# Keeping a split weight for a second use, and moving 24 matmuls ahead: two edits to a two-layer hybrid trunk

## The chip, the core and the metric

The kernel runs on one core of one Trainium2 chip. The metric is the device time of one launch in microseconds (us); lower is better. The engines of the core are TensorE (PE, matmuls), VectorE (DVE), ScalarE (ACT), GpSimd (POOL) and SyncE (SP, which issues the DMA loads). Each works through its own list of instructions in the order in which the program was built.

## The reference, cut to what matters

Two layers over 1024 rows of width 1024, everything in float32. Each layer is a token mixer (layer 0: a state-space mixer, layer 1: a short gated convolution) and then an MLP; each sub-layer is normalised, shifted, scaled, gated and added to the residual stream.

```
def short_conv_mixer(h, in_w, conv_w, out_w):
    proj = h @ in_w
    Bg, Cg, xv = jnp.split(proj, 3, axis=-1)
    y = Bg * causal_dwconv(Cg * xv, conv_w)
    return y @ out_w

def sqrelu_mlp(h, up_w, down_w):
    a = jax.nn.relu(h @ up_w)
    return (a * a) @ down_w
...
        h = rmsnorm(x, mlp_norm_w[i]) * (1.0 + sc_f) + sh_f
        x = x + g_f * sqrelu_mlp(h, mlp_up[i], mlp_down[i])
```

`mlp_up` is 1024 x 4096, `mlp_down` 4096 x 1024.

## The kernel before, in words

**Precision.** A float32 product is made of three matmuls: weight high part times activation high part, weight low part times activation high part, and a bf16 copy of the weight times the activation's low part. So each 128-column strip of a weight (a `wraw` tile, 128 x 1024, loaded by SP) is split in three: `split3` (L776) does a cast on ACT (`whi`, L783), a subtraction on DVE (`wlo`, L784) and a second cast on ACT (`wbf`, L785). The rings hold two `whi`, two `wlo`, two `wbf` and three `wraw`. A second helper, `split3h` (L788), does the same in two halves of 512 columns (L797 on ACT, L798 on DVE, L799 on ACT) and puts the high and low parts, four tiles of 128 x 512 for one strip, into the ring tagged `hh` in pool `mp`, which has 20 places; before the change only the last stages of the down projections use it.

**Halves.** The 1024 rows are handled as two halves of 512. The first half's activations of a sub-layer are ready before the previous sub-layer has ended; those of the second half come last, since the previous sub-layer's last results are theirs.

**The MLP's start.** `mlp` (L1068) works through 16 pairs of weight strips. For pairs 2 to 15 it uses a scheme with seven products in place of eight, which needs sums and differences of the activation blocks, named T1 to T4, of both halves. Pairs 0 and 1 are done plainly, in two steps: `plain_a` (L985) with the first half's rows (blocks B11 and B21), 24 matmuls to a strip, and then `plain_b` (L1002) with T1 and B22, 48 matmuls to a pair, whose weights are loaded and split again. Between the two stands `next(more)`, which emits T2 to T4. Then come `do_a(2)` and `do_a(3)` (24 matmuls each, L1016), `do_d(0)` and `do_d(1)` (down projection, 96 matmuls each; L870 adds the result to x on DVE).

**The second half's blocks.** `combos` (L881) makes them. Its first part is emitted before `mlp` begins: the norm of the second half (L245 to L265: a transpose on PE, the sum `na` on DVE L247, an inverse square root by small DVE operations, a broadcast matmul `bc` L265), then for each of four blocks a scaled block `nt` (L313, DVE), the high part of B22 (L906, ACT), its low part (L907, DVE), a difference (L909 on DVE, L910 on POOL), and T1's high part (L897, ACT) and low part (L898, POOL). The high parts are 8 tiles of the ring `hh`. The second part makes T2 to T4, 12 more tiles of `hh`, by L918 and L897/L898.

**Order.** Nobody writes the order of an engine's list: a tile scheduler does, by when an instruction's inputs and its buffer are there and by priorities. The second half's blocks have priority 500, T2 to T4 150, splits 200 (in `plain_b` 1000).

**The short convolution** has the same two steps: `unit(0,(0,))` and `unit(1,(0,))` for the first half of the first pair, `next(more)`, then `unit(0,(1,))` and `unit(1,(1,))`, and then `both(1)` to `both(3)` by the seven-product scheme. `both` begins with `part_a` (L1016) for the C columns: 24 matmuls that need only the first half's rows.

Of the kernel before, what the change touches and what calls it, by code (L numbers as in the profile page):

```python
# [16 lines left out]
P = 128  # L17
D = 1024
T = 1024
KT = D // P  # L20
TH = 512
# [11 lines left out]
def tile_trunk(ctx, tc, x, c, ada_w, ada_b, mix_norm_w, mlp_norm_w, mlp_up, mlp_down,  # L33
# [452 lines left out]
    with tc.tile_pool(name="ssd", bufs=2, reuse_waits="tile") as sp:  # L486
# [5 lines left out]
        W = ssd_in_w[0]  # L492
# [283 lines left out]
    def split3(raw, pri=None):  # L776

        w = raw.shape[-1]
        hi = wp.tile([P, 1024], F32R, tag="whi", name=nm("whi"), bufs=2)
        lo = wp.tile([P, 1024], F32R, tag="wlo", name=nm("wlo"), bufs=2)  # L780
        b = mp.tile([P, 1024], BF16, tag="wbf", name=nm("wbf"), bufs=2)
        with tc.high_priority(offset=pri or 200):
            A.copy(hi[:, :w], raw)  # L783
            V.tensor_tensor(out=lo[:, :w], in0=raw, in1=hi[:, :w].bitcast(F32), op=ALU.subtract)  # L784
            A.copy(b[:, :w], raw)  # L785
        return hi, lo, b
# [195 lines left out]
                parts("T4", hp, box0, T4)  # L982
        yield

    def plain_a(w, c0, H, tags):  # L985

        made = []
        for e in range(2):
            w3 = split3(raw_n(w, c0 + e * P))
            p1 = bank("mm", "mm")  # L990
            mul(p1, w3, LO4, H["B11"])
            m1 = mt("m1", 3) if tags[e] == "m1" else mt("sq", 1, tmp)
            A.copy(m1, p1)
            p2 = bank("mm", "mm")
            mul(p2, w3, HI4, H["B21"])
            c = mt("t", 3)
            with tc.high_priority(offset=500):
                V.tensor_tensor(out=c, in0=p2, in1=m1, op=ALU.add)
            made.append((c, m1))
        return made  # L1000

    def plain_b(w, c0, H, ms):  # L1002

        w1, w2 = split3(raw_n(w, c0), 1000), split3(raw_n(w, c0 + P), 1000)
        ps = [bank("sp", "mm") for _ in range(2)]
        for i in range(4):
            for p, (hi, lo, b) in zip(ps, (w1, w2)):
                for o, (ah, al_) in ((LO4[i], H["T1"][i]), (HI4[i], H["B22"][i])):
                    PE.matmul(p, lhsT=hi[:, o:o + P], rhs=ah, start=(i == 0 and o == LO4[i]), stop=False)
                    PE.matmul(p, lhsT=lo[:, o:o + P], rhs=ah, start=False, stop=False)  # L1010
                    PE.matmul(p, lhsT=b[:, o:o + P], rhs=al_, start=False, stop=(i == 3 and o == HI4[i]))
        for p, m1 in zip(ps, ms):
            V.tensor_tensor(out=m1, in0=p, in1=m1, op=ALU.add)
        return ms
# [53 lines left out]
    def mlp(l, H, more, after, mid, bg=iter(())):  # L1068
        n, LA = FF // 256, 3
        aa = {}  # L1070
        m1s = {}

        def relu2(c):
            V.scalar_tensor_tensor(out=c, in0=c, scalar=0.0, in1=c, op0=ALU.max, op1=ALU.mult)
            return c

        def do_a(i):
            c, m1s[i] = part_a(mlp_up[l], i * 256, H)
            aa[i] = [[keep("a1", relu2(c)), None], [None, None]]

        def do_b(i):
            for (f, hf), c in zip(((0, 1), (1, 1), (1, 0)), part_b(mlp_up[l], i * 256, H, m1s.pop(i))):
                aa[i][f][hf] = keep("ab", relu2(c))

        def do_d(i):
            for _ in second(mlp_down[l], i * 256, 1, [aa.pop(i)], l, 5):
                for _ in range(2 if i else 1):
                    next(bg, None)

        half = {}  # L1090
        NP = 2
        for i in range(NP):
            half[i] = plain_a(mlp_up[l], i * 256, H, ("m1", "m1" if i == 0 else "sq"))
            aa[i] = [[None, None], [None, None]]
            for f in range(2):
                aa[i][f][0] = keep(("a1", "ab")[f], relu2(half[i][f][0]))
        next(more)
        for i in range(NP):
            for f, c in enumerate(plain_b(mlp_up[l], i * 256, H, [h[1] for h in half.pop(i)])):
                with tc.high_priority(offset=200):  # L1100
                    aa[i][f][1] = keep("ab", relu2(c))
        do_a(2)
        do_a(3)
        do_d(0)
        do_d(1)
        do_b(2)
        do_a(4)
        steady[0], turn_[0] = True, 0
        for i in range(2, n - 1):
            do_b(i + 1)  # L1110
            if i < n - 2:
                do_d(i)
                if i + LA < n:
                    do_a(i + LA)
        steady[0] = False
        run(bg)
        run(second(mlp_down[l], (n - 2) * 256, 2, [aa[n - 2], aa[n - 1]], l, 5, PARTS if l else HALVES, after, mid))
# [8 lines left out]
    def short_conv(H, more, mid):  # L1126
        W = sc_in_w[0]
        aa = {}

        def tap(ct, hf, v, o):  # L1130

            h = schalo[:, ct, :]
            A.activation(o, v, AF.Copy, scale=scw(2, ct))
            for k in range(2):
                d = 2 - k
                V.scalar_tensor_tensor(out=o[:, d:], in0=v[:, :TH - d], scalar=scw(k, ct), in1=o[:, d:],
                                       op0=ALU.mult, op1=ALU.add)
                if hf:
                    V.scalar_tensor_tensor(out=o[:, :d], in0=h[:, k:], scalar=scw(k, ct), in1=o[:, :d],
                                           op0=ALU.mult, op1=ALU.add)  # L1140
            if hf == 0:
                PL.tensor_copy(h, v[:, TH - 2:])

        def unit(ct, halves):
            acts = [H["B11"] + H["B21"], H["B12"] + H["B22"]]
            wc = split3(raw_n(W, D + ct * P))
            cg, cv = {}, {}
            for hf in halves:
                ps = bank("mm", "mm")
                mul(ps, wc, ALL8, acts[hf])  # L1150
                cg[hf] = mt("m1", 3)
                A.copy(cg[hf], ps)
            wx = split3(raw_n(W, 2 * D + ct * P))
            for hf in halves:
                px = bank("mm", "mm")
                mul(px, wx, ALL8, acts[hf])
                v = mt("t", 3)
                V.tensor_tensor(out=v, in0=px, in1=cg[hf], op=ALU.mult)
                o = mt("nt", 2, tmp)
                tap(ct, hf, v, o)  # L1160
                cv[hf] = o
            wb = split3(raw_n(W, ct * P))
            for hf in halves:
                pb = bank("mm", "mm")
                mul(pb, wb, ALL8, acts[hf])
                o = cv[hf]
                V.tensor_tensor(out=o, in0=pb, in1=o, op=ALU.mult)
                aa.setdefault(ct // 2, [[None, None], [None, None]])[ct % 2][hf] = \
                    keep("a1" if hf == 0 and ct % 2 == 0 else "ab", o)

        def both(p):

            ct = 2 * p
            pos = ((0, 0), (0, 1), (1, 1), (1, 0))
            cg = [mt(t, b, q) for t, b, q in (("adacc", 1, tmp), ("sq", 1, tmp), ("dg", 1, tmp), ("m1", 3, mp))]
            _, m1 = part_a(W, D + ct * P, H, cg[0])
            part_b(W, D + ct * P, H, m1, cg[1:])

            def gated(i, v):
                V.tensor_tensor(out=v, in0=v, in1=cg[i], op=ALU.mult)  # L1180
                f, hf = pos[i]
                tap(ct + f, hf, v, cg[i])

            v0, m1 = part_a(W, 2 * D + ct * P, H)
            gated(0, v0)
            c12, c22, c21 = part_b(W, 2 * D + ct * P, H, m1)
            gated(1, c12)
            gated(3, c21)
            gated(2, c22)

            def out(i, r):
                f, hf = pos[i]
                V.tensor_tensor(out=r, in0=r, in1=cg[i], op=ALU.mult)
                aa.setdefault(p, [[None, None], [None, None]])[f][hf] = keep("a1" if i == 0 else "ab", r)

            r0, m1 = part_a(W, ct * P, H)
            out(0, r0)
            for i, r in zip((1, 2, 3), part_b(W, ct * P, H, m1)):
                out(i, r)

        unit(0, (0,))
        unit(1, (0,))
        next(more)
        unit(0, (1,))
        unit(1, (1,))
        H.pop("B12")
        next(more)
        for p in range(1, 4):
            both(p)
            steady[0], turn_[0] = True, 0  # L1210
            if p < 3:
                run(second(sc_out_w[0], (p - 1) * 256, 1, [aa[p - 1]], 1, 2))
        steady[0] = False
        run(second(sc_out_w[0], 512, 2, [aa[2], aa[3]], 1, 2, HALVES, square, mid))
# [73 lines left out]
```

## Time and profile before

| what | value |
|---|---|
| median of 3 runs | 2637.76 us (2637.1 to 2641.67) |
| profiled execution: its own time | 2639.83 us |
| profiled execution: span of the trace | 2637.9 us |
| PE busy | 2507.8 us, 95% of the span |
| DVE busy | 2036.4 us, 77% |
| ACT busy | 1227.9 us, 47% |
| POOL busy | 583.7 us, 22% |
| mean clock of PE that the chip granted | 0.984 of full speed |

The span is what the trace covers, and the execution's own time is 1.9 us longer. PE is busy nearly all the time, so the 5% in which it is not are where time could be won, and they lie in a few places. Times of the trace below count from the span's start. The MLP of layer 0 begins at about 854 us, the short convolution's second half is at about 1625 us, and the MLP of layer 1 begins at about 1926 us.

### The profile page before, as it was taken

The page shows a single profiled execution, that of the slowest core. Times are in us where ns is not written, and L with a number is a line of the kernel's source. Part 1 is how long each engine was busy: PE and PEld are TensorE (multiplying, and loading weights), DVE is VectorE, ACT ScalarE, POOL GpSimd, SP SyncE. Part 2 cuts the span into 40 slices and gives each one's busy share as a digit, 9 for nine tenths or more (in the row PEclk, how much of TensorE's full clock was granted, in tenths as well). Part 3 has the DMA queues.
Part 4 walks back from the last instruction along what each step waited for, and adds up shares of the span by engine and source line. Part 5 has one row for each costly group of instructions (what it writes and reads, how often), then busy time and mean ns, then how long its engine had stood idle before and what let it go on. Part 6 is the DMA issues. An engine that isn't in the chain of part 4 may idle for free. (4 is left out here: it accounts for less than half of the span.)

```text
span 2637.9 us, 31678 instructions
## 1 busy us (share of the span) xinstructions
PE 2507.8 (95%) x11562; PEld 1745.2 (66%) x11562; DVE 2036.4 (77%) x3080; ACT 1227.9 (47%) x2262; POOL 583.7 (22%) x461
## 2 busy tenths in 40 slices
PE   7999999999998899999999998999988999999998
PEld 5777777877776456666666654666554666666666
DVE  7788797897898987878778679765798666666666
ACT  3676575675574524333333345534453343333434
POOL 3221120111121522122122103332234211122120
PEclk9999999999999899999999999999999999999999
DMA  8444344444541233333333212222221221222222
GB/s 241 139 141 140 116 120 121 129 127 141 147 144 56 69 97 106 117 119 106 120 100 116 65 56 72 72 64 72 65 64 49 64 65 55 72 64 64 72 62 75
DMA packets 332412, 256.26 MB, mean 97 GB/s; under 512 B 8824, under 2 KB 289104, under 8 KB 332256
## 3 DMA queue, kind: packets, MB, share of 16 engines
q1 hardware_dynamic: 332000, 254.12, 32.3%
q8 instruction: 90, 1.47, 0.2%
q14 instruction: 66, 0.54, 0.1%
q0 software_dynamic: 256, 0.12, 0.0%
HBM read 249.75 MB, written 4.46 MB: 96 GB/s over the span
## 5 line engine op out<-in xcount | busy, mean ns | idle before, releaser
L870 DVE SCALAR_TENSOR_TENSOR x<-mm,mod,x 128x512 f32<-128x512 f32 (+1 forms) x536 | 387.2, 739 | 138.3 <-PE mm L826 137.3
L826 PEld LDWEIGHTS <-wbf 128*128 128x128 bf16 x2268 | 192.6, 98 | 344.0 <-issue 195.5
L826 PE MATMUL mm<-hh,whi 128*128 128x512 f32 x1196 | 369.1, 427 | 22.7 <-ACT whi L783 8.6
L826 PE MATMUL mm<-ah,wlo 128*128 128x512 f32 (+1 forms) x1072 | 390.0, 427 | 0.0
L826 PE MATMUL mm<-ah,whi 128*128 128x512 f32 (+1 forms) x1072 | 366.0, 432 | 18.8 <-DVE x L870 14.0
L826 PE MATMUL mm<-hh,wlo 128*128 128x512 f32 x1196 | 369.7, 415 | 10.5 <-DVE wlo L784 10.4
L826 PE MATMUL mm<-hl,wbf 128*128 128x512 bf16 x1196 | 318.8, 385 | 4.7 <-ACT wbf L785 4.7
L826 PE MATMUL mm<-al,wbf 128*128 128x512 bf16 (+1 forms) x1072 | 312.2, 383 | 3.3 <-DVE x L870 3.1
L826 PEld LDWEIGHTS mm<-hh,whi 128*128 128x128 f32 x1196 | 230.0, 193 | 72.4 <-ACT hh L956 12.5
L826 PEld LDWEIGHTS mm<-hh,wlo 128*128 128x128 f32 x1196 | 226.5, 190 | 69.4 <-DVE wlo L784 15.0
L208 PE MATMUL mm<-hh,whi 128*128 128x512 f32 x616 | 248.9, 404 | 0.0
L210 PE MATMUL mm<-hl,whi 128*128 128x512 f32 x616 | 245.8, 399 | 0.0
L209 PE MATMUL mm<-hh,wlo 128*128 128x512 f32 x616 | 244.1, 396 | 0.0
L826 PEld LDWEIGHTS mm<-ah,whi 128*128 128x128 f32 x1072 | 204.8, 192 | 59.0 <-DVE x L870 17.1
L826 PEld LDWEIGHTS mm<-ah,wlo 128*128 128x128 f32 x1072 | 204.2, 190 | 53.0
L784 DVE TENSOR_TENSOR wlo<-wraw,whi 128x1024 fp32r<-128x1024 f32 x139 | 177.3, 1285 | 67.3 <-ACT whi L783 66.9
L783 ACT CAST whi<-wraw 128x1024 fp32r<-128x1024 f32 x139 | 144.0, 1047 | 129.1 <-PE mm L826 116.1
L785 ACT CAST wbf<-wraw 128x1024 bf16<-128x1024 f32 x139 | 143.7, 1043 | 120.0 <-PE mm L826 115.6
L1036 POOL TENSOR_TENSOR ws<-wraw 128x512 f32<-128x512 f32 x37 | 49.8, 1345 | 495.4 <-DMA wraw<-in_mlp_up_dram 475.7
L208 PEld LDWEIGHTS mm<-hh,whi 128*128 128x128 f32 x616 | 116.3, 189 | 30.1 <-issue 6.8
L209 PEld LDWEIGHTS mm<-hh,wlo 128*128 128x128 f32 x616 | 116.5, 189 | 27.2 <-issue 3.8
L210 PEld LDWEIGHTS mm<-hl,whi 128*128 128x128 f32 x616 | 116.4, 189 | 26.7 <-issue 3.0
(390 smaller groups left out, 4398.5 us busy)
## 6 DMA issues: line engine op xcount, KB each, us to landing
wraw<-in_mlp_up_dram SPq DMA_DIRECT2D x100, 512.0 KB, 3.9
adaw<-in_ada_w_dram SPq DMA_DIRECT2D x96, 512.0 KB, 4.0
wraw<-in_ssd_in_w_dram SPq DMA_DIRECT2D x82, 512.0 KB, 3.8
wdraw<-in_mlp_down_dram SPq DMA_DIRECT2D x64, 512.0 KB, 3.7
wraw<-in_sc_in_w_dram SPq DMA_DIRECT2D x39, 512.0 KB, 3.6
L<-da SPq DMA_DIRECT2D x32, 512.0 KB, 5.2
wdraw<-in_ssd_out_w_dram SPq DMA_DIRECT2D x32, 512.0 KB, 3.5
E<-de SPq DMA_DIRECT2D x56, 128.0 KB, 4.1
```

What stands on the lines that cost most here:

```text
L208: PE.matmul(ps, lhsT=hi[:, o:o + P], rhs=ah, start=(k == 0), stop=False)
L209: PE.matmul(ps, lhsT=lo[:, o:o + P], rhs=ah, start=False, stop=False)
L210: PE.matmul(ps, lhsT=hi[:, o:o + P], rhs=al_, start=False, stop=(k == nk - 1))
L783: A.copy(hi[:, :w], raw)
L784: V.tensor_tensor(out=lo[:, :w], in0=raw, in1=hi[:, :w].bitcast(F32), op=ALU.subtract)
L785: A.copy(b[:, :w], raw)
L826: PE.matmul(ps, lhsT=at((hi, lo, b)[j], offs[i]), rhs=blocks[i][j // 2], start=(e == 0), stop=(e == len(js) - 1))
L870: V.scalar_tensor_tensor(out=xv, in0=ps, scalar=g, in1=xv, op0=ALU.mult, op1=ALU.add)
L1036: PL.tensor_tensor(out=s1, in0=a21, in1=a22, op=ALU.add)
```

## The change

In both MLPs, pair 0's strips are split with `split3h`, and the split tiles are kept in a list `kept` from `plain_a` to `plain_b`, which then doesn't load and split them again. In the short convolution, `part_a` of `both(1)` (24 matmuls and the addition behind them) is emitted ahead of `next(more)` and the second half's units, and its result stands in a `t` tile instead of `adacc`.

```
-    def plain_a(w, c0, H, tags):
+    def plain_a(w, c0, H, tags, kept=None):
...
-            w3 = split3(raw_n(w, c0 + e * P))
+            w3 = (split3 if kept is None else split3h)(raw_n(w, c0 + e * P))
+            if kept is not None:
+                kept.append(w3)
...
-    def plain_b(w, c0, H, ms):
-
-        w1, w2 = split3(raw_n(w, c0), 1000), split3(raw_n(w, c0 + P), 1000)
+    def plain_b(w, c0, H, ms, kept=None):
+
+        w1, w2 = kept or (split3(raw_n(w, c0), 1000), split3(raw_n(w, c0 + P), 1000))
...
-        half = {}
+        half, kept = {}, []
...
-            half[i] = plain_a(mlp_up[l], i * 256, H, ("m1", "m1" if i == 0 else "sq"))
+            half[i] = plain_a(mlp_up[l], i * 256, H, ("m1", "m1" if i == 0 else "sq"), kept if i == 0 else None)
...
-            for f, c in enumerate(plain_b(mlp_up[l], i * 256, H, [h[1] for h in half.pop(i)])):
+            for f, c in enumerate(plain_b(mlp_up[l], i * 256, H, [h[1] for h in half.pop(i)], kept if i == 0 else None)):
...
+        early = {}
+
+        def begin(p):
+
+            early[p] = part_a(W, D + 2 * p * P, H, mt("t", 3))
+
         def both(p):
...
-            cg = [mt(t, b, q) for t, b, q in (("adacc", 1, tmp), ("sq", 1, tmp), ("dg", 1, tmp), ("m1", 3, mp))]
-            _, m1 = part_a(W, D + ct * P, H, cg[0])
+            cg = [None] + [mt(t, b, q) for t, b, q in (("sq", 1, tmp), ("dg", 1, tmp), ("m1", 3, mp))]
+            if p in early:
+                cg[0], m1 = early.pop(p)
+            else:
+                cg[0] = mt("adacc", 1, tmp)
+                _, m1 = part_a(W, D + ct * P, H, cg[0])
...
         unit(0, (0,))
         unit(1, (0,))
+        begin(1)
         next(more)
```

The order that the scheduler makes of it changes on several engines. The first place is ACT at the start of layer 0's MLP. Before, the splits of pair 0 (`whi_8049`, `whi_8087`) and of pair 1 (`whi_8135`) stand among the last squares of the norm (`sq`), ahead of the first cast of the second half's blocks, `hh_7999`:

```order
672 L783 CAST whi_8049<-wraw_8047 128x1024
673 L326 ACTIVATE hh_7789<-nt_7787,mod_138 128x512
...
677 L785 CAST wbf_8051<-wraw_8047 128x1024
678 L783 CAST whi_8087<-wraw_8085 128x1024
...
683 L783 CAST whi_8135<-wraw_8133 128x1024
...
690 L906 ACTIVATE hh_7999<-nt_7997,mod_138 128x512
691 L783 CAST whi_8303<-wraw_8301 128x1024
```

Of the change, at the same place; `dhi` and `dbf` are the high parts and bf16 copies that `split3h` makes of pair 0's strips, `whi_8145` and `whi_8183` are pair 1's splits:

```order
672 L783 CAST whi_8145<-wraw_8143 128x1024
...
677 L799 CAST dbf_8053<-wraw_8047 128x512 x2
...
683 L783 CAST whi_8183<-wraw_8181 128x1024
684 L785 CAST wbf_8185<-wraw_8181 128x1024
685 L906 ACTIVATE hh_7999<-nt_7997,mod_138 128x512
686 L897 CAST hh_8005<-nt_7995 128x512
...
692 L897 CAST hh_8044<-nt_8034 128x512
693 L797 CAST dhi_8049<-wraw_8047 128x512
694 L797 CAST dhi_8050<-wraw_8047 128x512
```

The bf16 copies and pair 1's splits stand early, but the high parts of pair 0 have moved behind all eight casts of the second half's blocks (685 to 692).

The second place is PE at the same point of the program. Before, the first matmuls of pair 0 follow directly on the last one of the mixer's output projection (L210), and the norm's transposes and broadcasts come some 30 rows later:

```order
3057 L210 MATMUL mm_7940<-yll,whi_7919 128x512
3058 L826 MATMUL mm_8055<-hh_7756,whi_8049 128x512
3059 L826 MATMUL mm_8055<-hh_7756,wlo_8050 128x512
3060 L826 MATMUL mm_8070<-hh_7778,whi_8049 128x512
3061 L826 MATMUL mm_8070<-hh_7778,wlo_8050 128x512
```

Of the change, with the transposes of the second half's norm (L245) and its broadcasts (L265) first:

```order
3057 L210 MATMUL mm_7940<-yll,whi_7919 128x512
3058 L245 MATMUL nps_7957<-ident,acc_7818 128x128 x4
3059 L265 MATMUL bc_7988<-dg_7989,ones_r 128x512
3060 L265 MATMUL bc_7988<-dg_7992,ones_r 128x512
3061 L826 MATMUL mm_8060<-hh_7756,dhi_8049 128x512
3062 L826 MATMUL mm_8060<-hh_7756,dlo_8051 128x512
```

Pair 0's matmuls now stand behind the broadcasts and read `dhi` and `dlo`; pair 1's stand behind pair 0's, as before. The MLP of layer 1 shows the same two shifts.

The third place is DVE in the short convolution, where the low part of the moved strip (`wlo_13711`) and the addition behind its matmuls (`t_13707`) now stand among the operations of the second half's blocks (L945, L951, L957):

```order
1869 L945 SCALAR_TENSOR_TENSOR hl_13473<-nt_13476,mod_139,hh_13478 128x512
1870 L784 TENSOR_TENSOR wlo_13711<-wraw_13708,whi_13710 128x1024
...
1882 L957 TENSOR_TENSOR hl_13752<-dg_13746,hh_13757 128x512
1883 L951 TENSOR_TENSOR adacc_13766<-adacc_13766,hl_13440 128x512
1884 L1033 TENSOR_TENSOR t_13707<-mm_13731,m_2575_13729 128x512
```

Before, that strip's low part stood at row 1919 and the addition at row 1936, behind them.

## Rows read from the trace of the kernel before

**Rows 1.** Windows: length, busy us of PE, PEld, DVE, ACT, POOL, PE clock, DMA share, GB/s.
```profile
853.80:877.60 23.80, 23.46 (x103) 13.33 (x102) 21.04 (x40) 14.98 (x20) 3.55 (x3) 1.00 0.38 109
877.60:911.00 33.40, 25.31 (x94) 14.12 (x93) 32.35 (x31) 14.35 (x20) 22.40 (x16) 0.85 0.17 50
911.00:930.60 19.60, 14.12 (x54) 8.37 (x53) 19.60 (x18) 10.17 (x14) 13.88 (x10) 0.91 0.26 77
930.60:959.00 28.40, 24.70 (x98) 13.81 (x96) 25.66 (x37) 7.58 (x11) 2.82 (x2) 0.88 0.28 87
...
1625.00:1656.00 31.00, 18.50 (x61) 10.13 (x60) 30.72 (x38) 11.41 (x18) 12.98 (x8) 0.78 0.17 51
```

**Rows 2.** What PE waited for from 853.8 to 959 us: total, times, longest.
```profile
PE mm L1010 <- DVE wlo L784: 5.5, 2, 3.9
PE mm L826 <- DVE x L870: 3.7, 1, 3.7
PE mm L826 <- ACT whi L783: 2.9, 1, 2.9
PE mm L1009 <- ACT whi L783: 2.5, 1, 2.5
PE mm L826 <- DVE wlo L784: 1.7, 1, 1.7
PE mm L826 <- ACT m L1022: 0.9, 1, 0.9
```

**Rows 3.** Timeline of PE: the MLP's first matmul, and two after a wait.
```profile
853.81 0.39 PE L826 MATMUL mm<-hh,whi 128*128 128x512 f32 x1
...
943.23 0.63 PE L826 MATMUL mm<-ah,wlo 128*128 128x512 f32 x1
943.66 0.65 PE L826 MATMUL mm<-al,wbf 128*128 128x512 bf16 x1
```

**Rows 4.** Timeline of DVE: the last additions to x of do_d(0), in both MLPs.
```profile
958.53 1.57 DVE L870 SCALAR_TENSOR_TENSOR x<-mm,mod,x 128x512 f32<-128x512 f32 x2
...
2031.73 0.75 DVE L870 SCALAR_TENSOR_TENSOR x<-mm,mod,x 128x512 f32<-128x512 f32 x1 [0.32 <-PE mm L826]
```

**Rows 5.** Timeline of DVE: from the norm's sum to the first block, in both MLPs.
```profile
860.28 0.69 DVE L247 TENSOR_REDUCE na<-nps 128x4 f32<-128x512 f32 x1 [0.75 <-PE nps L245]
...
861.55 1.22 DVE L784 TENSOR_TENSOR wlo<-wraw,whi 128x1024 fp32r<-128x1024 f32 x1
...
869.29 1.40 DVE L313 SCALAR_TENSOR_TENSOR nt<-x,smul,bc 128x512 f32<-128x512 f32 x2
...
1937.18 0.69 DVE L247 TENSOR_REDUCE na<-nps 128x4 f32<-128x512 f32 x1
...
1946.97 1.41 DVE L313 SCALAR_TENSOR_TENSOR nt<-x,smul,bc 128x512 f32<-128x512 f32 x2 [0.19 <-PE bc L265]
```

**Rows 6.** Timeline of ACT in layer 1's MLP: a split's casts, and the eighth block cast.
```profile
1931.33 1.05 ACT L783 CAST whi<-wraw 128x1024 fp32r<-128x1024 f32 x1 [1.15 <-PE mm L826]
...
1962.78 0.62 ACT L897 CAST hh<-nt 128x512 fp32r<-128x512 f32 x1 [1.94 <-POOL nt L910]
```

**Rows 7.** Timeline of all engines around 880.5 us.
```profile
880.31 1.17 POOL L910 TENSOR_TENSOR nt<-nt,hl 128x512 f32<-128x512 f32 x1 [0.63 <-DVE nt L909]
...
880.81 1.75 DVE L784 TENSOR_TENSOR wlo<-wraw,whi 128x1024 fp32r<-128x1024 f32 x1
```

**Rows 8.** Lines L797 and L798: duration ns min/median/max, first and last start.
```profile
L797 ACT CAST dhi<-wdraw x12: 612/618/622, 1511.7 to 2580.7; 128x512 fp32r<-128x512 f32 x12
...
L798 DVE TENSOR_TENSOR dlo<-wdraw,dhi x12: 679/684/693, 1512.3 to 2581.9; 128x512 fp32r<-128x512 f32 x12
```

**Rows 9.** What PE waited for from 1925.8 to 2031.6 us.
```profile
PE mm L826 <- ACT whi L783: 5.7, 1, 5.7
PE mm L826 <- DVE x L870: 4.2, 1, 4.2
...
PE mm L826 <- DVE wlo L784: 1.4, 2, 0.9
```

More of the change, by code (lines that the diff above doesn't have):

```diff
@@ L1000, in plain_a, with at @@
         return made
-    def plain_b(w, c0, H, ms):
-        w1, w2 = split3(raw_n(w, c0), 1000), split3(raw_n(w, c0 + P), 1000)
+    def plain_b(w, c0, H, ms, kept=None):
+        w1, w2 = kept or (split3(raw_n(w, c0), 1000), split3(raw_n(w, c0 + P), 1000))
+        def at(t, o):
+            return t[o // TH][:, o % TH:o % TH + P] if isinstance(t, list) else t[:, o:o + P]
         ps = [bank("sp", "mm") for _ in range(2)]
@@ L1008, in plain_b @@
                 for o, (ah, al_) in ((LO4[i], H["T1"][i]), (HI4[i], H["B22"][i])):
-                    PE.matmul(p, lhsT=hi[:, o:o + P], rhs=ah, start=(i == 0 and o == LO4[i]), stop=False)
-                    PE.matmul(p, lhsT=lo[:, o:o + P], rhs=ah, start=False, stop=False)
-                    PE.matmul(p, lhsT=b[:, o:o + P], rhs=al_, start=False, stop=(i == 3 and o == HI4[i]))
+                    PE.matmul(p, lhsT=at(hi, o), rhs=ah, start=(i == 0 and o == LO4[i]), stop=False)
+                    PE.matmul(p, lhsT=at(lo, o), rhs=ah, start=False, stop=False)
+                    PE.matmul(p, lhsT=at(b, o), rhs=al_, start=False, stop=(i == 3 and o == HI4[i]))
         for p, m1 in zip(ps, ms):
```

## The prediction, made before the changed kernel ran

> **What bounds the kernel now.** The page comes first: PE is busy 95% of the span, so the question is what ends the waits in the other 5%. The table of windows shows it for layer 0's MLP [rows 1]. From 853.8 to 877.6 us PE is full (103 matmuls in 23.80 us, one each 0.231 us): this is `plain_a` with the first half's rows, while DVE, ACT and POOL make the second half's norm and blocks beside it. From 877.6 to 911.0 DVE is full instead (32.35 of 33.40 us), and PE stands or runs at a lower clock; from 911.0 to 930.6 DVE has no idle time at all (19.60 of 19.60). What PE waits for is read from the list of waits [rows 2]: low and high parts of splits, which come late from a full DVE and ACT, then `m`, then results added to x. After its longer waits PE also restarts at 1.2 GHz, half its full clock: two matmuls stand 0.43 us apart there [rows 3]. Two such stretches, each of about 13 matmuls at 0.43 in place of 0.231, cost some 2.7 us each. The MLP of layer 1 is alike [rows 9]. In the short convolution's second half DVE is full too (30.72 of 31.00 us) while PE has only 61 matmuls [rows 1].
>
> So the first half's work, which needs nothing of DVE's late blocks, is the cover under which the second half's blocks are made. A change that gives DVE less to do in the full stretch gains; one that takes the cover away loses it.
>
> **The change part by part.**
>
> *What it removes, in each MLP.* Two loads of 512 KB: worth nothing, since DMA is at 0.17 to 0.38 in these windows [rows 1] and PE's list of waits names no load [rows 2]. Two low parts of 1.22 us on DVE [rows 5] and four casts of 1.05 us on ACT [rows 6], of `plain_b`. In DVE's full stretch that is 2.4 us, and with it the waits of `plain_b` for pair 0's splits could go (a part of the 5.5 and 2.5 of L1010 and L1009 [rows 2]).
>
> *What it moves: pair 0's split.* Its eight high and low tiles now come from the ring `hh`, which the second half's blocks use as well. In the order built of the change, the four `dhi` casts stand behind all eight casts of B22 and T1 on ACT, and the four `dlo` behind them on DVE. PE has the norm's transposes and broadcasts first, then pair 0's matmuls, then pair 1's. Pair 1's splits come early, but its matmuls stand behind pair 0's and can't use them. So PE has nothing to do from the end of the mixer until the last block is cast. That is the cover, gone: some 24 us of matmuls that used to lie under the blocks.
>
> The Trainium skill says the same of the lists ("PSUM — Partial Sum Buffer", section "Engine vs sequencer instructions"): the queues of ScalarE and VectorE are strict first-in first-out, and matmuls start and complete in program order, so neither the `dhi` casts nor pair 1's matmuls can pass what stands ahead. It is the rule that speaks most against this change; if engines could pass a waiting instruction, pair 1's 48 matmuls would start where they did and about 11 us of each loss would go. No row of before has such a queue to show it.
>
> *When the first matmul comes, layer 0.* The norm's sum `na` stays at 860.3, and the first block `nt` comes 9.0 us later at 869.3 [rows 5]. In between DVE also does six operations of `plain_a`, two of 1.22 (such as the one at 861.55) and four of 0.69, in all 4.7 us of its time; they are not ready any more in the change. About 1.1 us of that filled gaps in which the norm's chain of small operations waited for itself, so the chain takes about 5.4 us, and `nt` comes at 865.7. From `nt` to the end of the eighth cast I take layer 1's time, where PE and DVE are laid out alike: from 1946.97 [rows 5] to 1962.78 + 0.62 [rows 6] is 16.4 us, of which a split (1.13 us of DVE's time) and an addition (0.6) of `plain_a` fall away, which leaves 14.7. So the casts end at 880.4, and `dhi` (0.62 us, rows of the same helper [rows 8]) lets PE start at 881.0, 27 us later than the 853.81 of before [rows 3].
>
> The first `dlo` (0.68 us [rows 8]) may come later still. DVE's operations with two inputs in SBUF end when a POOL operation does: a low part of 1.22 us took 1.75 beside POOL's `nt`, and ended about 1.1 us after it [rows 7]. I take no extra for it; a microsecond or two would come on top. The Trainium skill ("SBUF — State Buffer", section "🔬 SBUF: two separate sides") calls it an exclusive lock, held for a whole instruction by whichever of the two begins first, where a plain sharing of the port would stretch both; the row's 1.75 fits a wait ahead of an unchanged 1.22. It would not change the sum.
>
> *How much of it comes back.* From the MLP's start to the end of `do_d(0)` PE has 96 matmuls of `plain_a`, 96 of `plain_b`, 48 of `do_a` and 96 of `do_d(0)`: 336 by 0.231 = 77.6 us. Before they took from 853.8 to the sixteenth addition at 959.2 (the second of the two from 958.53 [rows 4]), 105.4 us: 27.8 were waits and low clock. In the change the matmuls begin late, and all the waits for pair 0's split are behind them. Against 77.6 I add two restarts at half clock (5.4: one after the long pause, one later, as before), the waits of `do_a` for its own splits and `m` (2.9 + 1.7 + 0.9 = 5.5 [rows 2]) and that of `do_d` for x (3.7 [rows 2]): DVE still has T2 to T4 and these to do. That ends at 881.0 + 77.6 + 5.4 + 5.5 + 3.7 = 973.2, which is **+14.0**.
>
> The bounds: with no wait and one restart (2.7) it ends at 961.3, +2.1. DVE would allow this only if it were never idle: from 881 on it has 74.2 us of its 77.6 in the last three of the MLP's windows [rows 1], less two low parts (2.4), plus four `dlo` (2.7) and four operations of `plain_a` that used to lie ahead (2.8), together 77.3 us, as much as PE has. Two engines that wait for each other can't both be full, so I take the upper sum. With four microseconds more of port waits and 4 more of ring waits it would be +22.
>
> *Layer 1's MLP.* ACT no longer has the two 1.05 us casts of a split [rows 6] among the norm's squares, which brings `na` from 1937.2 to about 1935.2. Then by the same steps: `nt` at 1940.7, the casts' end at 1955.4, PE's start at 1956.0, and 77.6 + 5.4 + (5.7 + 1.4) + 4.2 [rows 9] to 2050.3, against 2031.7 before [rows 4]: **+18.6**; bounds +4.6 and +24.
>
> *The short convolution.* The 24 matmuls are 24 x 0.231 = 5.5 us, need the first half's rows only, and fill a stretch where PE has 12 us and more of nothing [rows 1]. On the other side the low part (1.13 of DVE's time) and the addition (0.6) now stand among the blocks that bound the stretch, and delay them by 1.7. Filling less delay is 5.5 - 1.7 = 3.8; part of it is lost since the matmuls come before the longer waits and not in them. I take **-3**; bounds -6 (one half-clock restart fewer) and +1.7.
>
> *The sum.* +14.0 + 18.6 - 3 = +29.6. The profiled execution would go from 2639.8 to 2669.4; it stands 2.1 above the median, so the median goes from 2637.8 to **2667 us**.
>
> **The rivals.**
> - *Recovery.* Nothing but the late start is lost: +2.1 + 4.6 - 3 = +3.7, 2641.5 us. For it: all the old waits for splits were DVE's and ACT's lateness, and by 881 us these have caught up. Against: the 77.3 us of DVE above. Chance 0.12.
> - *The other side: the waits of `plain_b` were worth more than the cover.* It needs the first matmul by about 870 us, that is, the `dhi` casts between the block casts, or `plain_a`'s matmuls done while the last blocks are made. Then the two low parts and the waits for pair 0's split go (2.4 to 4 us in each MLP), with -3 in the short convolution: about 2629 us. It decides at a start of some 868 us in layer 0. Against it stands the built order, which can't be passed. Chance 0.04.
> - *The ring runs dry.* Of 20 places in `hh` eight hold pair 0's split until `plain_b(0)` has ended and eight hold B22 and T1; only four are left for the twelve tiles of T2 to T4. The rest of T2 to T4 then begins after 881.0 + 144 x 0.231 = 914 us, and if the seven-product work of pair 2 waits for it, some 5 us more come in each MLP: 2677 us. Chance 0.12.
> - *Nothing changes*, since loads and splits were hidden and the scheduler's order evens out: 2638 us. Chance 0.03; the built order moves too much.
>
> **How the numbers follow.** The forecast has 0.69. What a measurement of this kernel can tell from no change is about 0.2%, 5.3 us. Faster is the second rival, 0.04; within 0.2% are the fourth and about two thirds of the first, 0.11; slower is the rest, 0.85. The range goes from 2645, which leaves out the lower cases, to 2684, the upper bounds of the MLPs in part together: 0.8.
>
> **What would show it.** In the profile after: no L826 matmul with `dhi` in layer 0's MLP before about 880 us, and one wait of PE of over 15 us there, put down to `dhi` or `dlo`; PE at low clock right behind it; the waits of L1010 for `wlo` less than the 5.5 of before; in the short convolution 24 more matmuls ahead of the stretch that DVE fills. It is wrong if PE's start lies below 870 us, or if `do_d(0)` ends within 5 us of 959.

## The result, and the profile after

The changed kernel takes 2669.25 us (median of 4 runs, 2664.58 to 2673.17) against 2637.43 before: a ratio of 1.0116, 95% interval 1.0104 to 1.0129. It is 1.2% slower. Its profiled execution took 2669.97 us, with a span of 2668.0. The page's head shows PE with about as much work as before and a larger span:

```profile
span 2668.0 us, 31539 instructions
PE 2501.9 (94%) x11425; PEld 1748.0 (66%) x11562; DVE 2018.5 (76%) x3080; ACT 1221.6 (46%) x2262; POOL 579.6 (22%) x461
PEclk9999999999998899999999999999979999999999
```

DVE and ACT are busy 17.9 and 6.3 us less than before; the four removed low parts are 4.9 of the 17.9. The span still went up by 30.1 us, so the loss is waiting.

Where it lies is seen from three stretches that each begin and end with an addition to x on DVE (L346 for layer 0's mixer, L870 for the rest), read from the timeline of DVE in each profile. "Layer 0's MLP" goes from the mixer's last addition to the first of `do_d(0)`, "short convolution" from layer 0's last addition to the first of the short convolution, "layer 1's MLP" from the short convolution's last addition to the first of `do_d(0)`:

| kernel | layer 0's MLP | short convolution | layer 1's MLP |
|---|---|---|---|
| before | 85.2 | 146.1 | 82.3 |
| changed | 101.5 | 142.9 | 99.7 |
| difference | +16.3 | -3.2 | +17.4 |

The three differences add up to 30.5, as much as the span's 30.1; smaller differences around them nearly cancel. In layer 1 about 4 us come back around the stretch: the short convolution's last additions take 42.4 us in place of 44.6, and from the last addition of `do_d(1)` to the first of `do_d(2)` it is 38.8 us in place of 40.4. About as much is lost outside the stretches, the largest part of it, some 2 us, at the end of layer 0's mixer (see "When PE starts" below).

What PE waited for in layer 0's MLP, 853 to 980 us, of the changed kernel (total, times, longest):

```profile
PE mm L826 <- ACT dhi L797: 16.3, 1, 16.3
PE bc L265 <- DVE nrl L255: 5.6, 1, 5.6
PE nps L245 <- DVE acc L224: 4.8, 1, 4.8
PE mm L826 <- ACT whi L783: 3.9, 1, 3.9
PE mm L826 <- DVE dlo L798: 2.0, 1, 2.0
PE mm L826 <- ACT m L995: 1.1, 1, 1.1
```

All but the 3.9 are new: PE waits for the norm's sum, for its inverse root, for all eight block casts and the `dhi` behind them, for `dlo`, and for an `m` tile of `plain_a` (L995). The waits of before [rows 2] are nearly all gone; of 17.2 us in those six rows only the one for `do_a`'s high part is left, at 3.9 where it was 2.9. The timeline of PE shows the end of the pause and the low clock behind it:

```profile
885.94 0.80 PE L826 MATMUL mm<-hh,dhi 128*128 128x512 f32 x1 [16.33 <-ACT dhi L797]
888.72 0.80 PE L826 MATMUL mm<-hh,dlo 128*128 128x512 f32 x1 [1.98 <-DVE dlo L798]
...
890.19 0.63 PE L826 MATMUL mm<-hh,dlo 128*128 128x512 f32 x1
890.62 0.65 PE L826 MATMUL mm<-hl,dbf 128*128 128x512 bf16 x1
```

Two neighbours stand 0.43 us apart, as after the waits of before [rows 3]. The timeline of ACT shows what stood ahead of `dhi`:

```profile
884.75 0.62 ACT L897 CAST hh<-nt 128x512 fp32r<-128x512 f32 x1 [2.23 <-POOL nt L910]
885.28 2.17 ACT L797 CAST dhi<-wraw 128x512 fp32r<-128x512 f32 x4
```

The four `dhi` casts run directly on the eighth block cast, as the built order has it. The windows of the changed kernel (length, busy us of PE, PEld, DVE, ACT, POOL, then PE clock, DMA share, GB/s):

```profile
853.80:885.90 32.10, 4.59 (x11) 2.34 (x10) 24.30 (x41) 12.68 (x20) 9.90 (x8) 0.55 0.12 33
885.90:911.00 25.10, 21.91 (x78) 11.79 (x80) 20.06 (x22) 6.62 (x13) 15.61 (x11) 0.86 0.15 42
911.00:957.30 46.30, 42.31 (x176) 25.00 (x177) 33.44 (x42) 21.88 (x31) 15.28 (x10) 0.96 0.26 74
957.30:976.90 19.60, 19.60 (x86) 11.36 (x87) 16.27 (x24) 4.25 (x5) 0.00 (x0) 1.00 0.38 123
1944.40:1972.60 28.20, 2.70 (x7) 1.31 (x7) 22.70 (x40) 7.32 (x13) 9.97 (x8) 0.56 0.00 0
```

Against the first of the windows before, where PE had 103 matmuls in 23.80 us [rows 1], it now has 11 in 32.1. From 911.0 on DVE is no longer full (33.44 of 46.30), and PE is: the bound has gone from DVE to PE, but after a pause in which neither had enough to do.

### The profile page after: what moved, and what is told of

It reads as the page before. It is cut to its first block, busy times and chain, and to the rows that moved or that the text cites. A ratio compares the mean times of both kernels' runs of the same rounds, so it can differ in the third digit from the quotient of the medians.

```text
span 2668.0 us, 31539 instructions
## 1 busy us (share of the span) xinstructions
PE 2501.9 (94%) x11425; PEld 1748.0 (66%) x11562; DVE 2018.5 (76%) x3080; ACT 1221.6 (46%) x2262; POOL 579.6 (22%) x461
## 5 line engine op out<-in xcount | busy, mean ns | idle before, releaser
L870 DVE SCALAR_TENSOR_TENSOR x<-mm,mod,x 128x512 f32<-128x512 f32 (+1 forms) x536 | 387.3, 740 | 139.7 <-PE mm L826 138.2
L826 PEld LDWEIGHTS <-wbf 128*128 128x128 bf16 x2236 | 189.1, 98 | 335.2 <-issue 187.0
L826 PE MATMUL mm<-ah,wlo 128*128 128x512 f32 (+1 forms) x1072 | 389.1, 426 | 0.0
L826 PE MATMUL mm<-ah,whi 128*128 128x512 f32 (+1 forms) x1072 | 363.7, 430 | 10.8 <-DVE x L870 6.1
L826 PE MATMUL mm<-hh,wlo 128*128 128x512 f32 x1164 | 358.1, 416 | 10.4 <-DVE wlo L784 10.3
L826 PE MATMUL mm<-hh,whi 128*128 128x512 f32 x1164 | 350.1, 423 | 17.4 <-ACT whi L783 7.8
L826 PE MATMUL mm<-al,wbf 128*128 128x512 bf16 (+1 forms) x1011 | 295.7, 382 | 6.7 <-DVE x L870 4.3
L826 PE MATMUL mm<-hl,wbf 128*128 128x512 bf16 x1097 | 294.8, 386 | 7.4 <-ACT wbf L785 4.2
L826 PEld LDWEIGHTS mm<-hh,whi 128*128 128x128 f32 x1164 | 222.9, 192 | 66.6 <-ACT whi L783 8.8
L826 PEld LDWEIGHTS mm<-hh,wlo 128*128 128x128 f32 x1164 | 221.5, 191 | 68.6 <-DVE wlo L784 14.6
L208 PE MATMUL mm<-hh,whi 128*128 128x512 f32 x616 | 249.6, 405 | 0.0
L210 PE MATMUL mm<-hl,whi 128*128 128x512 f32 x616 | 246.3, 400 | 0.0
L209 PE MATMUL mm<-hh,wlo 128*128 128x512 f32 x616 | 244.7, 397 | 0.0
L826 PEld LDWEIGHTS mm<-ah,wlo 128*128 128x128 f32 x1072 | 204.0, 190 | 52.7 <-issue 0.3
L826 PEld LDWEIGHTS mm<-ah,whi 128*128 128x128 f32 x1072 | 203.8, 191 | 50.2 <-DVE x L870 8.7
L784 DVE TENSOR_TENSOR wlo<-wraw,whi 128x1024 fp32r<-128x1024 f32 x131 | 166.1, 1278 | 68.0 <-ACT whi L783 67.1
L783 ACT CAST whi<-wraw 128x1024 fp32r<-128x1024 f32 x131 | 135.7, 1048 | 122.9 <-PE mm L826 104.6
L785 ACT CAST wbf<-wraw 128x1024 bf16<-128x1024 f32 x131 | 135.4, 1044 | 120.8 <-PE mm L826 115.4
L208 PEld LDWEIGHTS mm<-hh,whi 128*128 128x128 f32 x616 | 116.6, 189 | 30.3 <-issue 6.8
L210 PEld LDWEIGHTS mm<-hl,whi 128*128 128x128 f32 x616 | 116.6, 189 | 26.7 <-issue 3.0
```

The lines of the kernel that those rows point to most:

```text
L208: PE.matmul(ps, lhsT=hi[:, o:o + P], rhs=ah, start=(k == 0), stop=False)
L209: PE.matmul(ps, lhsT=lo[:, o:o + P], rhs=ah, start=False, stop=False)
L210: PE.matmul(ps, lhsT=hi[:, o:o + P], rhs=al_, start=False, stop=(k == nk - 1))
L826: PE.matmul(ps, lhsT=at((hi, lo, b)[j], offs[i]), rhs=blocks[i][j // 2], start=(e == 0), stop=(e == len(js) - 1))
L870: V.scalar_tensor_tensor(out=xv, in0=ps, scalar=g, in1=xv, op0=ALU.mult, op1=ALU.add)
```

## The experiments

All variants are made from the changed kernel. `e8` was run once; the others were timed in alternation with the kernel before. The stretches of each profile, as above:

| run | edit | ratio to before, 95% interval | layer 0's MLP | short conv. | layer 1's MLP |
|---|---|---|---|---|---|
| e1 | short convolution's edit alone | 0.9986 (0.9974 to 0.9998) | 85.2 | 142.3 | 82.3 |
| e2 | the MLPs' edit alone | 1.0107 (1.0090 to 1.0124) | 101.4 | 145.9 | 102.2 |
| e3 | kept, split emitted first | 0.9981 (0.9968 to 0.9994) | 86.0 | 142.2 | 78.7 |
| e4 | late split, not kept | 1.0170 (1.0150 to 1.0190) | 109.4 | 141.9 | 108.1 |
| e5 | pair 1 kept, not pair 0 | 1.0038 (1.0021 to 1.0055) | 88.7 | 141.9 | 89.9 |
| e6 | as e3, layer 1 only | 0.9978 (0.9964 to 0.9992) | 85.2 | 142.6 | 78.7 |
| e7 | as e3, one strip of two | 0.9996 (0.9982 to 1.0010) | 86.7 | 142.1 | 82.6 |
| e8 | split's priority 2000 | one run, span 2660.4 | 101.0 | 144.0 | 99.8 |
| e9 | e3, `do_a` splits raised | 0.9985 (0.9971 to 0.9999) | 84.7 | 143.0 | 79.1 |
| e10 | e6, `do_a` splits raised | 0.9973 (0.9962 to 0.9983) | 87.2 | 142.2 | 79.1 |

### e1 and e2: each edit alone

```
e1   w1, w2 = kept or (...)   ->   plain_a and plain_b get no list, both pairs split by split3
e2   -        begin(1)
```

> Only the short convolution's edit; both MLPs as before. My reading of the two traces (the stretch between the two MLPs is about 1.9 us shorter after the change): -1.5 to -3 us against the kernel before, 2634.5 to 2636 us. Rival, that the low part and the addition put among the second half's blocks cost what the 24 matmuls fill: no change, 2637 to 2638 us.

> Only the MLPs' edit; the short convolution as before. If the two edits simply add, this is the changed kernel plus what the short convolution's edit gains: +32 to +35 us against before, 2669.5 to 2672 us, with PE's pause at the start of each MLP as long as in the changed kernel (16.3 us before the first dhi matmul). Rival, that the short convolution's edit has a part in layer 1's loss: layer 1's MLP loses clearly less than 14 us here.

e1 has 2630.99 us against 2634.67, a ratio of 0.9986, 3.7 us less, a little more than the 1.5 to 3 expected; its short convolution takes 142.3 us, against 142.9 in the changed kernel and 146.1 before. e2 has a ratio of 1.0107, +28.2 us. The two make +24.5 us, where the changed kernel has +30.6 (1.0116); with intervals of 3 to 4.5 us to each side of each ratio that is no contradiction, and no proof that they add. The stretches say more: in e2 layer 0's MLP has 101.4 us and the short convolution 145.9, in e1 85.2 and 142.3, so neither edit reaches into the other's stretch there. Layer 1's MLP is 2.5 us longer in e2 than in the changed kernel (102.2 against 99.7), with the same start of PE and the same work of DVE behind it (54.74 and 54.72 us); what differs is the granted clock behind PE's start, 0.87 against 0.94. So a stretch of one profile can move by some 2.5 us, and smaller differences between stretches show little. The +32 to +35 expected of e2 was some 4 us too high.

### e3: the split emitted ahead of the second half's blocks

```
     more = combos(0, 3, mact, H0)
+    kept0 = pre(0)          # [split3h(raw_n(mlp_up[0], e * P)) for e in range(2)]
     next(more)
...
-            w3 = (split3 if kept is None else split3h)(raw_n(w, c0 + e * P))
+            w3 = split3(raw_n(w, c0 + e * P)) if kept is None else kept[e]
```

and the same in layer 1.

> The changed kernel, but pair 0's split is emitted ahead of the second half's blocks, so that its tiles are taken from the ring before theirs; the split is still kept for plain_b. Theory of the lost cover: dhi casts come ahead of the block casts, PE starts the MLP right behind the mixer, the loss of about 30 us goes, and what is left is the gain of two low parts and four casts per MLP and of the short convolution: 2626 to 2634 us. Rival of the ring: with eight places held by the kept tiles, four are left for T2 to T4, these come late, and the kernel stays 5 to 15 us above before. Rival, that the late start is not the reason: 2660 us or more.

2630.24 us against 2634.67, a ratio of 0.9981: the whole loss is gone, with the same tiles kept in the same ring for as long as `plain_b` needs them. The timeline of PE of this run shows pair 0's first matmul directly behind the mixer's last one:

```profile
855.34 0.39 PE L210 MATMUL mm<-yll,whi 128*128 128x512 f32 x1
855.57 0.40 PE L826 MATMUL mm<-hh,dhi 128*128 128x512 f32 x1
857.77 0.49 PE L826 MATMUL mm<-hh,dlo 128*128 128x512 f32 x1 [1.81 <-DVE dlo L798]
```

So it was the place of `dhi` and not the keeping, and the 2626 to 2634 us expected hold. Layer 1's MLP is 3.7 us shorter than before; layer 0's is not. The list of waits in layer 0's MLP of this run says where its gain went:

```profile
PE mm L826 <- ACT whi L783: 11.4, 1, 11.4
PE mm L826 <- DVE wlo L784: 3.1, 1, 3.1
PE mm L826 <- ACT sq L993: 2.9, 1, 2.9
...
PE mm L826 <- DVE dlo L798: 1.8, 1, 1.8
```

`plain_b`'s waits for pair 0's splits are gone, but PE then stands 11.4 us for the high part of `do_a`, where it stood 2.9 before [rows 2]. These waits together come to 19.2 us, against 17.2 in the six rows of before.

### e4: the late split without the keeping

```
-  plain_b(mlp_up[l], i * 256, H, [h[1] for h in half.pop(i)], kept if i == 0 else None)
+  plain_b(mlp_up[l], i * 256, H, [h[1] for h in half.pop(i)])
```

> The changed kernel, but plain_b loads and splits pair 0 again and lets the first split's tiles go after plain_a; only the helper and the ring of the first split differ from before. Theory of the lost cover: the dhi casts still stand behind the block casts, so it is as slow as the changed kernel or slower by up to the two low parts per MLP: 2669 to 2676 us. Rival, that holding eight places of the ring until plain_b has ended is what costs: 2640 to 2655 us.

2680.17 us, a ratio of 1.0170, slower than the changed kernel by about 0.5% and above the 2669 to 2676 that I expected, since I had put the second split at no more than its two low parts in each MLP. The pause is there unchanged, and the waits for a second split come on top (list of waits, layer 0's MLP):

```profile
PE mm L826 <- ACT dhi L797: 16.3, 1, 16.3
...
PE mm L826 <- ACT m L995: 4.7, 2, 3.7
PE mm L1016 <- DVE wlo L784: 2.8, 2, 2.4
...
PE mm L1015 <- ACT whi L783: 1.8, 1, 1.8
```

Layer 0's MLP takes 109.4 us and layer 1's 108.1, so in the changed kernel keeping the split is worth about 8 us in each (109.4 - 101.5, 108.1 - 99.7). The lateness alone costs three times that, 24.2 us (from 85.2) and 25.7 us (from 82.3).

### e5: pair 1's split kept in place of pair 0's

```
-  ... kept if i == 0 else None)
+  ... kept if i == 1 else None)        # in both calls, plain_a and plain_b
```

> The changed kernel, but pair 1's split is the kept one and pair 0 is split as before (and split again in plain_b). The dhi casts still stand behind the block casts, but pair 0's 48 matmuls (11.1 us) lie ahead of them. Theory of the lost cover: the pause of PE shrinks by those 11 us in each MLP, and the loss with it: MLP of layer 0 +4 to +8 us, of layer 1 +2 to +6, short convolution -3, in all +3 to +11 us against before. Rival, that it is the helper or the ring and not the matmuls under the blocks: as slow as the changed kernel, +30.

2646.18 us against 2635.66, a ratio of 1.0038: a third of the loss, with the 48 matmuls of one pair ahead of the late split in place of none. The loss, 10 us, lies in the range expected, but is split otherwise: layer 0's MLP loses 3.5 us in this stretch (4 to 8 expected) and layer 1's 7.6 (2 to 6). The lists of waits, first of layer 0's MLP (from 845 us), then of layer 1's (from 1910):

```profile
PE mm L1015 <- ACT hh L897: 5.2, 1, 5.2
PE mm L826 <- ACT m L1028: 3.0, 1, 3.0
PE mm L826 <- DVE wlo L784: 2.4, 1, 2.4
PE mm L826 <- ACT dhi L797: 2.0, 1, 2.0
```

```profile
PE mm L826 <- ACT dhi L797: 16.4, 1, 16.4
PE mm L826 <- DVE wlo L784: 4.7, 1, 4.7
```

In layer 0 the scheduler also put pair 0's `plain_b` (L1015) ahead of pair 1's `plain_a`, and PE works on the blocks as they come; its wait for `dhi` is 2.0 us. In layer 1 it is as long as in the changed kernel, since it begins behind the norm's broadcasts, but 48 matmuls are done before it. So layer 1 is the clean case: its loss is 9.8 us less than the changed kernel's 17.4, for matmuls of 11.1 us.

### e6 and e7: one layer only, one strip only

```
e6   kept0 = None                                       # layer 0's MLP as before
e7   return [split3h(raw_n(mlp_up[l], 0))]               # the second strip: split3, in plain_a and again in plain_b
```

> As the run with the split emitted first, but in layer 1 alone; layer 0's MLP as before, short convolution as in the change. By the stages of that run (layer 0's MLP +1.1 us, short convolution -3.9, layer 1's MLP -6.2): -9 to -10 us, a ratio of 0.996 to 0.997. Rival, that layer 1's -6.2 was chance of one profile: -3 to -4 us, a ratio of 0.9985.

> As the run with the split emitted first, in both layers, but only the first of pair 0's two strips is kept; the other is split as before and again in plain_b. Four places of the ring are held in place of eight, and eight are left for T2 to T4. Theory that the ring's shortage eats the gain: layer 0's MLP, where ACT's whi for do_a stood 11.4 us late behind casts of T2 to T4, gets 2 to 5 us shorter than with both strips kept, in all -8 to -12 us against before. Rival, that DVE's work and not the ring sets that stretch: one more low part in each MLP costs 1 to 3 us more than with both kept, in all -2 to -6 us.

e6 has 2627.53 us against 2635.66, a ratio of 0.9978. Layer 1's MLP takes 78.7 us again, so its gain was no chance of one profile; the ratio lies between the two expectations, and its interval reaches into both. e7 has 0.9996, by the ratio 1.1 us less than before, with an interval of some 4 us to each side: the theory's 8 to 12 lies outside it, the rival's 2 to 6 in part inside. Its layer 0 takes 86.7 us, against 86.0 with both strips kept: the four places of the ring that it frees bring nothing in this stretch, and the ring's shortage is not what eats layer 0's gain there. That theory of mine fell. In layer 1 it has 82.6, as before: there the gain showed only with both strips kept.

### e8: the priority of the split

```
-        with tc.high_priority(offset=200):
+        with tc.high_priority(offset=2000):            # split3h of pair 0 only
```

> The changed kernel with the priority of pair 0's split raised from 200 to 2000, above the 500 of the blocks. If the ring's order of allocation holds the dhi casts back, they stay behind the block casts and nothing changes: a span of 2666 to 2671 us. Rival, that the scheduler put them there by priority: PE starts the MLP 15 us or more earlier and the span is 2630 to 2645 us.

The span is 2660.4, below the range that I gave, and one run doesn't show whether that is more than chance. The stretches are the same to within 0.5 us (101.0 and 99.8), and so is PE's pause, 16.34 us:

```profile
882.53 0.80 PE L826 MATMUL mm<-hh,dhi 128*128 128x512 f32 x1 [16.34 <-ACT dhi L797]
```

With four times the priority of the blocks `dhi` still stands behind them, and with the split emitted ahead of the blocks (e3) it doesn't. The reading that fits both is that places in one ring are given in the order in which the program asks for them: the blocks ask for their eight places of `hh` first, so `dhi` gets its own after the last of them. It is a reading: the raised priority covers the casts and subtractions and not the requests for tiles, which stand ahead of it in `split3h`, and a raised request was not tried. The `dbf` copies, from another ring, and pair 1's splits, from the rings of `whi` and `wlo`, were not held.

### e9 and e10: the split of do_a raised

```
-        w3 = split3(raw_n(w, c0))                       # part_a
+        w3 = split3(raw_n(w, c0), pri)                  # pri = 1000 for do_a(2) and do_a(3)
```

> The run with pair 0's split emitted first in both layers, and with the priority of the splits of do_a(2) and do_a(3) raised from 200 to 1000. There PE stood 11.4 us (layer 0) and 8.2 us (layer 1) for whi of do_a, which ACT did behind casts of T2 to T4. In the built order whi moves ahead of one cast only, since its ring of two is held by plain_b(1). Theory that the order of these casts gives the gain back: 2 to 5 us shorter in layer 0's MLP (169.5 us with the split first). Rival, that DVE's work as a whole sets this stretch: within 1.5 us of 169.5.

> The best version so far (pair 0's split emitted first in layer 1 alone, layer 0's MLP as before, short convolution as in the change), with the same raised priority for do_a(2) and do_a(3) in both layers. If the order of the casts matters, 2 to 6 us below it, a ratio to before of 0.9955 to 0.997; if DVE's whole work sets both stretches, the same as it, 0.9975 to 0.998.

To the first addition of `do_d(2)`, the stretch that e9's expectation means, layer 0's MLP takes 167.3 us in e9, 2.2 less than the 169.5 of e3 and 1.0 less than the 168.4 of before. That is the lower end of the 2 to 5 expected, and no more than the clock alone moved a stretch in e2. PE's wait for `do_a`'s high part is still 10.4 us of the 11.4. The ratios are 0.9985 for e9 and 0.9973 for e10, and their intervals overlap those of e3 and e6. In e10 the raised splits shortened neither stretch (87.2 and 79.1, against 85.2 and 78.7 of e6). So this is undecided: in these runs the order of these casts was worth some 2 us at most. e10 has the best ratio of all, 0.9973 (0.9962 to 0.9983), and like e1, e3, e6 and e9 it beats both the kernel before and the changed one.

## Why the prediction was right, and what in it was not

**The cover.** Right, and shown from three sides: with the same keeping and an early split the loss is gone (e3); with a late split and no keeping it is larger (e4); with 48 matmuls ahead of the late split a third of it is left (e5). The step "PE has nothing to do from the end of the mixer until the last block is cast" is what the trace after shows, in one wait of 16.3 us and two of 5.6 and 4.8 for the norm. Pair 1's matmuls did not pass pair 0's: its splits were done at 865.5 us, and its `wlo` matmuls (L826) ran from 902.3 to 914.4.

**When PE starts.** 885.9 us against the 881.0 that I worked out. 1.7 us of it were lost ahead of the MLP, where my sum had nothing: the mixer's last addition is at 855.8, before at 854.0. The timeline of PE, first of the changed kernel, then of the kernel before:

```profile
851.10 0.50 PE L208 MATMUL mm<-yhl,whi 128*128 128x512 f32 x1 [2.23 <-DVE x L346]
...
853.07 0.63 PE L208 MATMUL mm<-yhl,whi 128*128 128x512 f32 x1
853.50 0.63 PE L209 MATMUL mm<-yhl,wlo 128*128 128x512 f32 x1
```

```profile
850.92 0.50 PE L208 MATMUL mm<-yhl,whi 128*128 128x512 f32 x1 [1.70 <-DVE x L346]
...
853.11 0.39 PE L208 MATMUL mm<-yhl,whi 128*128 128x512 f32 x1
853.34 0.40 PE L209 MATMUL mm<-yhl,wlo 128*128 128x512 f32 x1
```

PE's wait for x is 0.5 us longer, and the mixer's last matmuls behind it stand 0.43 us apart where they stood 0.23 apart: the granted clock is 0.50 from 852.0 to 855.4 us. The mixer's last addition comes 2.1 to 2.2 us behind the one before it in all six kernels that split both strips of layer 0's pair 0 by `split3h` (the changed one, e2, e3, e4, e8, e9), and 0.7 us in the other six, so these 2 us belong to the change. Why x comes later was not tested; on ACT the cast of pair 1's first strip there waits 0.55 us for its load. The rest of the 4.9 us is 3.2, most of it in one term. The timeline of DVE of the changed kernel:

```profile
861.68 0.69 DVE L247 TENSOR_REDUCE na<-nps 128x4 f32<-128x512 f32 x1 [1.21 <-PE nps L245]
...
864.30 1.23 DVE L784 TENSOR_TENSOR wlo<-wraw,whi 128x1024 fp32r<-128x1024 f32 x1 [0.34 <-ACT whi L783]
...
869.65 1.41 DVE L313 SCALAR_TENSOR_TENSOR nt<-x,smul,bc 128x512 f32<-128x512 f32 x2 [0.89 <-PE bc L265]
...
883.03 0.68 DVE L918 TENSOR_TENSOR nt<-hh,hh 128x512 f32<-128x512 f32 x1
...
886.32 1.75 DVE L918 TENSOR_TENSOR nt<-nt,hl 128x512 f32<-128x512 f32 x1 [1.05 <-POOL nt L918]
887.99 0.68 DVE L798 TENSOR_TENSOR dlo<-wraw,dhi 128x512 fp32r<-128x512 f32 x1
```

From `na` to the first block it is 8.0 us, not 5.4: one split of pair 1 (864.30) still stands in the chain, and the rest is the chain's own waiting, for `bc` of PE at its low clock among it. The operations of `plain_a` had filled gaps more than they had taken time. From `nt` to the end of the eighth cast it is 15.7 us, not 14.7, since a T2 operation (883.03) stands ahead of the last low part. Another (886.32) stands ahead of the first `dlo`, which is PE's wait of 2.0: the sum had taken no extra for it, though the prediction named a microsecond or two. It was also wrong there to say that DVE's operations end when a POOL operation does; its own row [rows 7] has the low part end 1.1 us later.

**How much comes back.** From PE's start to the sixteenth addition of `do_d(0)` I had 92.2 us; in the changed kernel it is 89.7 (885.94 to 975.68). So the late start was under-sized and the waits behind it over-sized, and the two partly cancel: 16.3 us later than the 959.3 of before, where I had +14.0. The waits behind the start are 7.0 us (3.9, 2.0 and 1.1) where I had 9.2 (5.5 + 3.7): `do_d`'s wait for x, 3.7, didn't come. The two restarts at half clock came, one right behind the pause (a granted clock of 0.86 in the second window) and one behind the wait of 3.9 at 941 us (0.83 from 940 to 950). The reason for taking the upper sum did not hold: from PE's start to 976.9 us DVE has 69.8 us of work (20.06 + 33.44 + 16.27) in place of the 77.3 that were to fill it as much as PE.

In layer 1 PE's start is well met: the short convolution's last additions begin 16.5 us later than before, and PE 16.6 us later than the 1956.0. From there to the sixteenth addition it is 91.1 us (1972.6 to 2063.6) where I had 94.3. Up to that addition layer 1 lost 15.4 us, with the 2.2 that came back ahead of the MLP, where I had +18.6, and 1.6 more come back later; the term that was too large is the carried-over waits of 5.7 + 1.4 + 4.2, of which the changed kernel has 3.9 for `do_a`'s split and 3.2 for a `t` tile, besides 2.0 for `dlo`.

That the total is nearer (+29.6 against 31.8 by the medians and 30.1 by the spans) than its parts is luck: one layer was put too low and the other too high.

**The rivals.** *Recovery* was half right: the waits for splits of before are mostly gone, and from 911.0 to 957.3 us DVE is at 33.44 of 46.30 us where I held it to be full. But the pause was longer than what went away. *The ring runs dry* was wrong: PE's list has no wait for a T2 to T4 cast in layer 0's MLP, and e7 shows the ring to matter little. *The other side* is what e3 makes of the change, and it is smaller than the 2629 us against 2637.8 that I gave it: of its 8.8 us, e3 shows 4.4 by its medians.

**The removed splits.** I gave the two low parts 2.4 us and their waits a part of 5.5 and 2.5. Under a late start they are worth 8 us (e4 against the changed kernel); under the old cover 3.7 us in layer 1 and nothing in layer 0 (e3), where PE waits for `do_a`'s split in place of `plain_b`'s.

**The short convolution.** -3 predicted, -3.2 in the stretch, and 0.9986 when it is the only edit. The lists of waits of that stretch, 1589 to 1732 us of the changed kernel:

```profile
PE mm L826 <- DVE wlo L784: 5.7, 4, 2.2
PE mm L826 <- ACT m L1158: 4.2, 2, 3.7
```

and 1569.7 to 1715.8 us of the kernel before:

```profile
PE mm L826 <- DVE t L1158: 6.3, 1, 6.3
PE mm L826 <- ACT hh L956: 5.7, 1, 5.7
PE mm L826 <- DVE wlo L784: 2.6, 3, 1.1
PE mm L826 <- ACT m L1022: 0.7, 1, 0.7
```

PE's waits go from 15.3 to 9.9 us. The two long ones shrink to one of 3.7, and those for low parts grow by 3.1: the moved low part stands in DVE's full stretch, as the sum had it. In e1, with the same edit, they grow by 0.7 only (3.3 us), so the size of this cost is not settled.

**What stays open.** Why the kept split gains 3.7 us in layer 1 and nothing in layer 0. DVE is busy 74.18 us of layer 1's stretch in e3 where it was 80.37 before, and 79.69 where it was 81.38 in layer 0, so DVE saves 6.2 us in the one and 1.7 in the other. That the time follows from this is argued and not shown, and what makes DVE's saving differ was not isolated. In this stretch the ring is not it (e7), and the order of `do_a`'s casts is some 2 us of it at most (e9). In layer 0 e3 also loses the 2 us at the mixer's end, ahead of the stretch; e7, which keeps one strip, does not.

## What to carry to other kernels

Work that needs nothing of a late stage is worth most at the moment when that stage is made: before a tile is kept or shared, ask which ring it comes from and who asks that ring first, since a split that waits for a place behind the late stage takes its matmuls with it. A removed load or cast is worth what waited for it: here 8 us in one order and nothing to 4 us in another. The built order tells the place of such a loss, and the rows of the trace before its size: here to within some 3 us in each MLP up to the point where the sum ended, in part because errors of both signs cancelled.

## What the runs showed that was not expected

Raising the split's priority to 2000 moved nothing (a pause of 16.34 us against 16.33), while the same split emitted ahead of the blocks removed the pause: in this kernel a place in a ring seems to have gone by the order of the program, not by the priority of the work. The same saving differed by a factor: two loads, two low parts and four casts of an MLP were worth about 8 us under the late start and 0 to 4 us under the early one. And the change reached back ahead of its own stage: a wait for x that grew by 0.5 us at the mixer's end brought some 2 us, with the last matmuls at half clock.
